# Both inputs loaded by halves of the batch: partition p holds rows 4p to 4p+3 of each half, and the result is stored in two parts

## The chip, the cores and the metric

One core of one Trainium2 chip. The time is the device time of a run in microseconds (us), without the profiler's own work; 84.16 us before the change (3 runs). A profiled execution has a "span" of its own, about 1.3 us shorter than the time of the run that it belongs to (82.9 us for a run of 84.24), because it starts with the first instruction and ends with the last. All runs quoted are in the fast state, at a granted clock of 1.00.

## The reference

```python
batch, dim = 1024, 4096            # x, y: float32
def reference(x, y, axis):         # axis = -1
    return np.sum((x - y) ** 2, axis=axis).astype(np.float32)
```

33.55 MB are read from HBM, the chip's main memory, and 4 KB are written to it.

## The kernel before

128 partitions (P), R = 8 rows each, N = 8 x 4096 columns per partition. X and Y are tiles in the on-chip memory. SP (SyncE) issues all loads into one queue; DVE (VectorE) subtracts, ACT (ScalarE) squares with a running sum, DVE adds up the sums of the pieces of a row ("parts"). The pieces get shorter towards the end, and the last one is squared on DVE itself, with an earlier part as the start value. The engines and the DMA (the transfers) tell each other of finished work by semaphores: counters that one raises and another waits for. The code is cut at the lines of dots.

```python
xv = x.rearrange("(p r) d -> p (r d)", p=P)      # partition p: rows 8p to 8p+7
yv = y.rearrange("(p r) d -> p (r d)", p=P)
ov = out.rearrange("(p r) -> p r", p=P)          # 8 results, 32 B, per partition
...
xw = [16384, 8192, 5472, 1280, 960, 320, 160]    # widths of the loads, in columns
yw = [16256, 8192, 2624, 2784, 1344, 480, 480, 288]
late, last = 128, 192                            # the last two loads of Y
LATE = 3                                         # the row whose end comes last
...
for j, (c0, c1) in enumerate(ys):
    final = j == len(ys) - 1
    wait_loaded(c1, landed_y[j][1])
    for piece in pieces_of(j, c0, c1):
        sub(*piece)                              # DVE
        ...
        if final:                                # DVE: square, add the start value, sum
            nc.vector.tensor_tensor_reduce(..., scalar=parts_of(r, 1),
                accum_out=results[:, r : r + 1]).then_inc(sums, 1)
            continue
        square(*piece, where[piece])             # ACT
        ...
    if j == 4:
        for r in (4, 5, 6):
            complete(r)                          # DVE: sum of the row's parts
complete(7)

nc.sync.wait_ge(sums, n["sums"])
nc.sync.dma_start(out=ov, in_=results).then_inc(stored, 16)
prog.close(nc.sync, stored, 16)                  # SP waits for the store
```

Of the kernel before, what the change touches and what calls it, by code (L numbers as in the profile page):

```python
# [47 lines left out]
def kernel(tc, x, y, axis, out):  # L48
    nc = tc.nc
    P = nc.NUM_PARTITIONS  # L50
    F32 = mybir.dt.float32
    Square = mybir.ActivationFunctionType.Square
    mult, add = mybir.AluOpType.mult, mybir.AluOpType.add

    B, D = x.shape
    R = B // P
    N = R * D


    xv = x.rearrange("(p r) d -> p (r d)", p=P)  # L60
    yv = y.rearrange("(p r) d -> p (r d)", p=P)
    ov = out.rearrange("(p r) -> p r", p=P)


    H = 6 * D
    X = nc.alloc_sbuf_tensor("X", [P, H], F32).ap()
    Y = nc.alloc_sbuf_tensor("Y", [P, H], F32).ap()
    results = nc.alloc_sbuf_tensor("results", [P, R], F32).ap()



    xw = [16384, 8192, 5472, 1280, 960, 320, 160]
    yw = [16256, 8192, 2624, 2784, 1344, 480, 480, 288]
    late, last = 128, 192
    LATE = 3
    halved = (1, 2, 3, 4)
    cut = (LATE + 1) * D - late
    assert sum(xw) == N and sum(yw) == N - late - last
    xs, c = [], 0
    for w in xw:  # L80
        xs.append((c, c + w))
        c += w
    ys, c = [], 0
    for w in yw:
        ys.append((c, c + w))
        c += w
        if c == cut:
            c += late
    ys += [(N - last, N), (cut, cut + late)]

    prog = Program(nc, tc)
    stored = nc.alloc_semaphore("stored")
    diffs = prog.semaphore("diffs")
    acts = prog.semaphore("acts")
    sums = prog.semaphore("sums")
    n = dict(diffs=0, acts=0, sums=0)

    def home(c0, c1):
        h0 = c0 % H
        return slice(h0, h0 + c1 - c0)  # L100


    landed_x, landed_y = [], []
    freed = []

    def load(landed, src, dst, name, c0, c1):
        sem = prog.semaphore("%s%d" % (name, len(landed)))
        nc.sync.dma_start(out=dst[:, home(c0, c1)], in_=src[:, c0:c1]).then_inc(sem, 16)  # L108
        landed.append(((c0, c1), sem))

    order = []
    have = 0
    for c0, c1 in ys:
        while have < c1:
            order.append((landed_x, xv, X, "x") + xs[len([o for o in order if o[3] == "x"])])
            have = order[-1][5]
        order.append((landed_y, yv, Y, "y", c0, c1))

    todo = list(order)
    for _ in range(2):  # L120
        load(*todo.pop(0))
    prog.early(mybir.EngineType.SP)
    while todo and todo[0][5] <= H:
        load(*todo.pop(0))


    row_parts = [[] for _ in range(R)]
    def pieces_of(j, c0, c1):

        pieces = []  # L130
        while c0 < c1:
            e = min(c1, (c0 // D + 1) * D)
            if j in halved:
                h = (c0 + e) // 64 * 32
                pieces.append((c0, h))
                c0 = h
            pieces.append((c0, e))
            c0 = e
        return pieces

    for j, (c0, c1) in enumerate(ys):
        for piece in pieces_of(j, c0, c1):
            row_parts[piece[0] // D].append(piece)
    parts, where = None, {}
    total = sum(len(p) for p in row_parts if len(p) > 1)
    parts = nc.alloc_sbuf_tensor("parts", [P, total], F32).ap()
    k = 0
    for r, p in enumerate(row_parts):
        for piece in p:
            where[piece] = parts[:, k : k + 1] if len(p) > 1 else results[:, r : r + 1]  # L150
            k += len(p) > 1
    first = {}
    k = 0
    for r, p in enumerate(row_parts):
        if len(p) > 1:
            first[r] = k
            k += len(p)

    def parts_of(r, m):
        return parts[:, first[r] : first[r] + m]  # L160

    seen_x = [0]

    def wait_loaded(c1, ysem):

        waits = []
        while seen_x[0] < len(xs) and xs[seen_x[0]][0] < c1:
            waits.append(seen_x[0])
            seen_x[0] += 1
        nc.vector.wait_ge(ysem, 16)  # L170
        for k in waits:
            nc.vector.wait_ge(landed_x[k][1], 16)

    def sub(c0, c1):
        a = X[:, home(c0, c1)]
        nc.vector.tensor_sub(out=a, in0=a, in1=Y[:, home(c0, c1)]).then_inc(diffs, 1)  # L176
        n["diffs"] += 1

    def square(c0, c1, acc):
        a = X[:, home(c0, c1)]  # L180
        nc.scalar.wait_ge(diffs, n["diffs"])
        nc.scalar.activation(out=a, in_=a, func=Square, accum_out=acc).then_inc(acts, 1)  # L182
        n["acts"] += 1

    squared = {}

    def complete(r):
        nc.vector.wait_ge(acts, squared[row_parts[r][-1]])
        nc.vector.tensor_reduce(  # L189
            out=results[:, r : r + 1],  # L190
            in_=parts_of(r, len(row_parts[r])),
            axis=mybir.AxisListType.X,
            op=add,
        ).then_inc(sums, 1)
        n["sums"] += 1
# [5 lines that stand above are left out]
            sub(*piece)  # L201
            r = piece[0] // D
            if final:
                nc.vector.wait_ge(diffs, n["diffs"])
                nc.vector.tensor_tensor_reduce(  # L205
                    out=Y[:, home(*piece)],
                    in0=X[:, home(*piece)],
                    in1=X[:, home(*piece)],
                    scale=1.0,
                    scalar=parts_of(r, 1),  # L210
                    op0=mult,
                    op1=add,
                    accum_out=results[:, r : r + 1],
                ).then_inc(sums, 1)
                n["sums"] += 1
                continue
            square(*piece, where[piece])
            squared[piece] = n["acts"]
            if r in (0, 1):

                nc.sync.wait_ge(acts, n["acts"])  # L221
                while todo and todo[0][5] <= H + (r + 1) * D:
                    load(*todo.pop(0))
                if r == 1:
                    while todo:
                        load(*todo.pop(0))
        if j == 4:
            for r in (4, 5, 6):
                complete(r)
    complete(7)  # L230

    nc.sync.wait_ge(sums, n["sums"])
    nc.sync.dma_start(out=ov, in_=results).then_inc(stored, 16)
    prog.close(nc.sync, stored, 16)


# [33 lines left out]
```

## Time and profile before

| | before |
|---|---|
| time, median of 3 | 84.16 us (84.10 to 84.48) |
| span of the profiled run | 82.9 us |
| DMA share of the span, 16 engines | 95.8% |
| last load landed (trace) | 80.53 us |
| final store issued, landed | 81.47, 82.87 us |

The prediction shows the lines of the profile and reads them. Its times from single DMA records (80.55, 82.89, and with it 1.42 for the store) lie up to 0.02 us above the zero of the profile's views; here they are given from that zero, and the store takes 1.41 us.

One more line matters later. After it has issued the store, SP clears its semaphores and waits for the store's completion. In the view of SP's own waits of the kernel before (columns: us in total, times, longest):

```profile
SPq L45 <- SPq L45: 1.0, 1, 1.0
```

So of the store's 1.4 us, 1.0 is spent in plain waiting at the very end of the program.

### The profile page before, as it was taken

The numbers are of one execution on the slowest core, as the hardware profiler recorded it, in microseconds if no ns is written. First come the engines' busy times: TensorE is split into PE (matmuls) and PEld (weight loads), VectorE is DVE, ScalarE is ACT, GpSimd is POOL, SyncE is SP. The second block draws the span as 40 slices with busy tenths as digits, with TensorE's granted clock in tenths as the row PEclk, the third lists the DMA queues.
The fourth block names the chain that finished last, engine by engine and source line by source line (L and its number), as shares of the span: only waits on it lengthen the run. The fifth ranks groups of instructions, "written<-read, shape, count | busy, mean of one in ns | idle before, by whom it ended". The sixth has DMA issues, their size and how long they took to land.

```text
span 82.9 us, 135 instructions
## 1 busy us (share of the span) xinstructions
DVE 36.9 (44%) x27; ACT 33.5 (40%) x41; POOL 0.2 (0%) x4
## 2 busy tenths in 40 slices
DVE  0000000000000000000299999999189996989992
ACT  0500000000000000000000979889886999899991
POOL 0000000000000000000000000000000000000000
DMA  9299999957999996599799979969989899999960
GB/s 506 95 411 506 506 506 506 474 221 316 502 502 502 502 502 282 220 502 502 316 443 506 427 332 506 490 269 506 411 348 496 369 405 438 430 403 421 396 214 2
DMA packets 2592, 33.56 MB, mean 405 GB/s; under 512 B 416, under 2 KB 1312, under 8 KB 1696
## 3 DMA queue, kind: packets, MB, share of 16 engines
q1 hardware_dynamic: 2592, 33.56, 95.8%
HBM read 33.55 MB, written 0.00 MB: 405 GB/s over the span
## 4 chain that ended last, share of the span: by engine, by line
DMA 64%; SPq 17%; DVE 12%; ACT 4%; issue 1%
DMA Y<-in_y_dram 64%; SPq L108 17%; DVE X L176 11%; ACT X L182 4%; DVE Y L205 0%; DVE results L189 0%; SPq L221 0%; DVE results L205 0%
## 5 line engine op out<-in xcount | busy, mean ns | idle before, releaser
L176 DVE TENSOR_TENSOR X<-X,Y 128x2048 f32<-128x2048 f32 (+10 forms) x21 | 36.3, 1779 | 44.5 <-DMA Y<-in_y_dram 44.4
L182 ACT ACTIVATE X<-X 128x2048 f32<-128x2048 f32 (+9 forms) x20 | 31.2, 1559 | 45.9 <-DVE X L176 45.8
L182 ACT ACTIVATION_READ_ACCUMULATOR X<-X 128x1 f32 x20 | 3.7, 186 | 0.0
L182 ACT ACT_TABLE_LOAD x1 | 1.3, 1283 | 1.9 <-PEq L19 1.9
L189 DVE TENSOR_REDUCE results<-parts 128x1 f32<-128x2 f32 (+2 forms) x4 | 0.4, 151 | 0.0
L205 DVE CUSTOM_DVE_ANT_0 Y<-X,parts 128x128 f32<-128x128 f32 x1 | 0.4, 353 | 0.0
L251 POOL MEMSET const-bfloat16-1.0<- 128x1 bf16 x1 | 0.1, 101 | 0.0
L251 POOL MEMSET const-uint8-127<- 128x1 uint8 x1 | 0.1, 101 | 0.0
L251 POOL MEMSET const-float32-0.0<- 128x1 f32 x1 | 0.1, 98 | 0.2 <-issue 0.2
L251 POOL MEMSET const-float32-1.0<- 128x1 f32 x1 | 0.1, 98 | 0.0
L205 DVE DVE_READ_ACCUMULATOR2_ANT results<- 128x1 f32 x1 | 0.1, 84 | 0.0
## 6 DMA issues: line engine op xcount, KB each, us to landing
Y<-in_y_dram SPq DMA_DIRECT2D x1, 8128.0 KB, 40.6
X<-in_x_dram SPq DMA_DIRECT2D x1, 4096.0 KB, 48.8
Y<-in_y_dram SPq DMA_DIRECT2D x1, 4096.0 KB, 58.2
X<-in_x_dram SPq DMA_DIRECT2D x1, 2736.0 KB, 13.4
Y<-in_y_dram SPq DMA_DIRECT2D x1, 1392.0 KB, 19.0
Y<-in_y_dram SPq DMA_DIRECT2D x1, 1312.0 KB, 16.2
Y<-in_y_dram SPq DMA_DIRECT2D x1, 672.0 KB, 21.2
X<-in_x_dram SPq DMA_DIRECT2D x1, 640.0 KB, 20.1
```

The costliest lines, as they stand in the source:

```text
L108: nc.sync.dma_start(out=dst[:, home(c0, c1)], in_=src[:, c0:c1]).then_inc(sem, 16)
L176: nc.vector.tensor_sub(out=a, in0=a, in1=Y[:, home(c0, c1)]).then_inc(diffs, 1)
L182: nc.scalar.activation(out=a, in_=a, func=Square, accum_out=acc).then_inc(acts, 1)
L189: nc.vector.tensor_reduce(out=results[:, r : r + 1], in_=parts_of(r, len(row_parts[r])), axis=mybir.AxisListType.X, op=add,).then_inc(sums, 1)
L205: nc.vector.tensor_tensor_reduce(out=Y[:, home(*piece)], in0=X[:, home(*piece)], in1=X[:, home(*piece)], scale=1.0, scalar=parts_of(r, 1), ...
L251: nc = _bacc.Bacc("TRN2", target_bir_lowering=False, num_devices=1)
```

## The change

The loads' pieces of a partition are to lie closer together in memory: the 16,384 columns that a partition gets from the first load of X and of Y are four whole rows, and those of partition p+1 now follow at once, so such a load reads 8 MB in one piece. The price is that the results of a partition are two runs (stretches of consecutive bytes) of 4 values, 16 B, rather than one of 8, 32 B. The first half is therefore stored ahead, behind the loads in the queue. With it row 5's end comes last in place of row 3's, for row 3 belongs to the half that is stored early.

```diff
-    xv = x.rearrange("(p r) d -> p (r d)", p=P)
-    yv = y.rearrange("(p r) d -> p (r d)", p=P)
-    ov = out.rearrange("(p r) -> p r", p=P)
+    M = N // 2
+    xv = x.rearrange("(h p r) d -> p h (r d)", h=2, p=P)
+    yv = y.rearrange("(h p r) d -> p h (r d)", h=2, p=P)
+    ov = out.rearrange("(h p r) -> h p r", h=2, p=P)
...
-    yw = [16256, 8192, 2624, 2784, 1344, 480, 480, 288]
-    LATE = 3
+    yw = [16384, 8064, 2624, 2784, 1344, 480, 480, 288]
+    LATE = 5
...
-        nc.sync.dma_start(out=dst[:, home(c0, c1)], in_=src[:, c0:c1]).then_inc(sem, 16)
+        nc.sync.dma_start(out=dst[:, home(c0, c1)], in_=src[:, c0 // M, c0 % M : c0 % M + c1 - c0]).then_inc(sem, 16)
...   # complete(r) and the final square: row 5's start value is the sum of its two earlier parts
+            if r == R // 2 - 1:
+                nc.sync.wait_ge(acts, n["acts"])
+                nc.sync.dma_start(out=ov[0], in_=results[:, 0 : R // 2]).then_inc(stored, 16)
         if j == 4:
             for r in (4, 5, 6):
                 complete(r)
+            nc.vector.wait_ge(sums, n["sums"])
...
-    nc.sync.dma_start(out=ov, in_=results).then_inc(stored, 16)
-    prog.close(nc.sync, stored, 16)
+    nc.sync.dma_start(out=ov[1], in_=results[:, R // 2 : R]).then_inc(stored, 16)
+    prog.close(nc.sync, stored, 32)
```

More of the change, by code (lines that the diff above doesn't have):

```diff
@@ L187, in complete @@
     def complete(r):
-        nc.vector.wait_ge(acts, squared[row_parts[r][-1]])
+        done = row_parts[r][:-1] if r == LATE else row_parts[r]
+        nc.vector.wait_ge(acts, squared[done[-1]])
         nc.vector.tensor_reduce(
-            out=results[:, r : r + 1],
-            in_=parts_of(r, len(row_parts[r])),
+            out=where[row_parts[r][-1]] if r == LATE else results[:, r : r + 1],
+            in_=parts_of(r, len(done)),
             axis=mybir.AxisListType.X,
@@ L209 @@
                     scale=1.0,
-                    scalar=parts_of(r, 1),
+                    scalar=where[piece],
                     op0=mult,
```

## The prediction

> **What bounds the kernel now.** I read four views of the profile, in this order: the page's shares and slices, the chain that ended last, the busy time by stretches of 2 us, and the order of time for the last 4 us.
>
> The page first. It shows whether an engine or the transfers fill the span.
>
> ```profile
> DVE 36.9 (44%) x27; ACT 33.5 (40%) x41; POOL 0.2 (0%) x4
> ...
> q1 hardware_dynamic: 2592, 33.56, 95.8%
> HBM read 33.55 MB, written 0.00 MB: 405 GB/s over the span
> ```
>
> No engine is busy for half of the span; the 16 DMA engines are for 95.8% of it. While busy they moved 405 / 0.958 = 423 GB/s. There is one queue and the inputs are read once, so there are no bytes to save.
>
> The chain says the same, and where the transfers stop setting the end:
>
> ```profile
> 0.43 40.58 DMA Y<-in_y_dram
> ...
> 67.69 12.66 DMA Y<-in_y_dram
> 80.34 0.02 issue
> 80.37 0.57 DVE X L176 x2
> 80.94 0.03 issue
> 80.96 0.35 DVE Y L205
> 81.32 0.01 DVE results L205
> 81.33 0.11 DVE results L189
> ```
>
> Between the two DMA lines the chain runs through compute and through the queue's issue. That part is not what bounds: the third X load was issued at 53.63, when the fourth Y load was still running (DVE waited for it until 60.52). So the queue had about 7 us of work left, and the DMA engines never ran dry. The end is transfers until 80.34, then about 1.1 us of DVE, then the store.
>
> The stretches (columns: length, busy us of DVE, ACT, POOL, clock, DMA share, GB/s):
>
> ```profile
> 8.00:10.00 2.00, 0.00 (x0) 0.00 (x0) 0.00 (x0) 1.00 1.21 524
> 28.00:30.00 2.00, 0.00 (x0) 0.00 (x0) 0.00 (x0) 1.00 1.20 520
> 48.00:50.00 2.00, 2.00 (x2) 1.37 (x3) 0.00 (x0) 1.00 0.91 393
> ```
>
> A transfer is booked by its records' own times, 2.4 us for 64 KB, so a 2 us stretch can show over 1; the quotient is what counts: 524/1.21 = 433, 520/1.20 = 433, 393/0.91 = 432 GB/s. The rate while busy is the same with the compute engines idle and with them busy. Single packet records agree: one of 65,536 bytes takes 2.42 us, 27.1 GB/s per engine, 433 for 16. Smaller packets fit bytes / 27.08 GB/s plus about 7.5 ns (5,120 B in 196 ns, 1,280 B in 55, 512 B in 27).
>
> What falls short of that line, summed over records and divided by 16 engines, is small: the first packet of each engine takes about 3.1 us in place of 2.42 (0.63 us), and some packets from 51 to 63 us take 5 to 19% longer (0.19 us per engine).
>
> The last 4 us:
>
> ```profile
> 78.25 0.27 DVE L189 TENSOR_REDUCE results<-parts 128x1 f32<-128x2 f32 x3
> ...
> 78.44 2.49 DVE L176 TENSOR_TENSOR X<-X,Y 128x480 f32<-128x480 f32 x5
> ...
> 80.96 0.35 DVE L205 CUSTOM_DVE_ANT_0 Y<-X,parts 128x128 f32<-128x128 f32 x1
> 81.06 0.18 ACT L182 ACTIVATION_READ_ACCUMULATOR X<-X 128x1 f32 x1
> 81.24 0.08 DVE L205 DVE_READ_ACCUMULATOR2_ANT results<- 128x1 f32 x1
> 81.28 0.16 DVE L189 TENSOR_REDUCE results<-parts 128x1 f32<-128x8 f32 x1
> 81.47 0.35 SPq L233 DMA_DIRECT2D out_dram<-results  x1
> ```
>
> DVE's last subtractions follow the landings (5 between 78.44 and 80.94, each starting within about 0.1 us of its load). The store is issued at 81.47 and lands at 82.89, 1.42 us later.
>
> **What the Trainium skill says.** (1) "DMA: Bandwidth & Descriptors", section "Bandwidth" (Where 436 GB/s comes from): 16 SBUF ports of 32 B at 850 MHz give 435 GB/s, and 16 MB loaded at 425. The trace agrees: 433 in steady state. If that ceiling is on the SBUF side, no order of the HBM addresses can raise it. (2) The same page, "Latency and other measured facts", row on HBM row pitch: with 16 KiB per partition, copies keep 207 GB/s per direction at a pitch of 512 KiB (214 being full) and lose at 2 MiB and above. It says nothing of 128 or 64 KiB; the trace shows no loss at 128 KB, so I expect none at 64 KB. (3) The same page, "Anatomy of one DMA": the end of a transfer is mostly the receipt of the write, not the bytes. The store of 4 KB with 1.42 us from issue to landing, its packets 7 to 9 ns each, agrees. (4) The same page, "Queues, rings and completion order": an engine consumes descriptors in ring order, and the semaphore's write waits for that engine's earlier writes only. A store queued behind the last load thus cannot hold up that load's semaphore; no run here shows it yet.
>
> **The change part by part.**
>
> *Addresses of the loads.* Bytes do not change: the Y loads are 16,384 and 8,064 columns in place of 16,256 and 8,192; their sum, 24,448, and all later widths stay. Packets: still 17 loads of 128, one per partition, none above 65,536 B. By the fit a load packet costs the same: change 0.00 us for the steady part. What can move is the 0.63 us of the first packets and the 0.19 us of slow ones. The first I take as start-up latency, which addresses don't alter. The second could be bank conflicts between the 16 engines. Then denser addresses may help: a saving of perhaps half, 0.1 us, or up to about 0.4 us if the engine that ends last had most of it (the last load's 16 completions are spread over 80.16 to 80.55).
>
> *First Y load 128 columns wider.* 65,536 against 65,024 B at 27.08 GB/s: lands 0.02 us later per packet, times 8 packets per engine, 0.15 us. DVE's start moves from 41.03 to 41.18. Its fourth subtraction is 4,096 wide (4.42 us) in place of 3,968 (4.28): +0.14. DVE had 2.19 us idle before 60.52, so both vanish; the second X and Y loads end at the same byte count, 49,024 columns, as before. The release of the third X load is 0.15 us later out of 7 us of slack. Two halves of row 5 become 1,984 in place of 2,048 wide: about 0.13 us less before DVE waits for the next load at 70.20. On the path: 0.
>
> *Row 5's end last, in place of row 3's.* The last load has 128 columns as before. One reduction of two parts for row 5 stays, but it writes a part rather than a result. The final fused square-and-sum reads that as its start value. Same count of instructions on the path: 0.57 + 0.35 + 0.11 us as before.
>
> *The new wait of DVE for its own reductions.* Before, the reductions of 78.25 to 78.52 overlap the next subtraction (starting 78.44). Now that must wait for the last reduction's semaphore: about 78.52 plus 0.05, so 0.13 us late. Carried on: subtraction of 480 columns (0.66) ends at 79.23, the next at 79.89 (79.78 before), that of 288 (0.46) at 80.35; the 192-column load lands at 80.36. The delay is used up 0.01 us before the path starts. Cost 0, at worst 0.1.
>
> *The store in two.* The first half is issued after all loads are (they are out at 67.69 + 3.36 = 71.05) and after row 3's squares, which ended at about 62. So its issue at about 71.1, some 0.35 us, or a few us if the queue is still full, is over long before 81.47. It adds 128 packets of 16 B, 8 per engine at about 9 ns, 0.07 us, behind the last load's. They run at about 80.3 to 80.7, while DVE works. The final store has 128 packets still, of 16 B rather than 32: 0.00, with perhaps ±0.1 for short writes sharing a line of memory. Waiting for 32 rather than 16 costs nothing, since the first half has landed by then (estimate: 80.6 + about 1 us = 81.6, before 82.9).
>
> Sum on the path: 0 (steady transfers) − 0.1 (conflicts) + 0 (DVE) + 0 (stores) = −0.1 us, from 84.16: **84.05 us**.
>
> **The rivals.** *A: the layout wins noticeably.* Reading 8 MB in one contiguous piece could remove all the slow packets and part of the start: at most 0.4 + 0.6 = 1.0 us, 83.1 us, 1.2%. For it: the slow packets exist, and the change seems made for it. Against it: over 90% of packets already sit at one duration to 0.1%, the mark of a fixed limit, not of memory conflicts. Even all of it stays inside 2%. *B: the denser pitch hurts.* 16 engines then read at steps of 4 partitions, 256 KB in place of 512 KB. If these met in fewer banks, a loss of 3% in the rate would be 2.4 us, 86.5 us. Against it: the skill's row has losses grow with the pitch, not shrink. *C: a contiguous source is cut into other packets.* If the first loads were merged and cut otherwise, packets and engines would change. Against it: the store before is contiguous on the HBM side as well, and ran as 128 packets of 32 B. *D: the tail gets longer.* If DVE's new wait reaches the last load, or the two stores meet, 0.1 to 0.4 us more: 84.2 to 84.5 us.
>
> **Range and chances.** Before ran from 84.10 to 84.48, so one median carries about 0.15 us. With −0.4 for a good part of A and +0.4 for D, the range is 83.6 to 84.5 us. Over 2% faster means below 82.5 us: 1.6 us less, more than all losses that I could find: 0.03. Over 2% slower means above 85.8, only B or C: 0.03. Within 2%: 0.94.
>
> **What would show it.** Right: DMA share near 96%; quotient of GB/s and share near 433; 2,720 packets (128 more); DVE waiting for the fourth Y load until about 60.5; the last load's wait ending at about 80.3; about 1.1 us of DVE behind it; a final store of about 1.4 us. Wrong: first packets clearly under 3.1 us, or a landing of the second Y load well before 60.5 (A); 64 KB packets over 2.45 us (B); another count of packets (C); the 192-column subtraction starting after its landing, or a final store of over 1.5 us (D).

## The result, and the profile after

The changed kernel is correct and takes 85.12 us in the median (84.97 to 85.55, 4 runs); before took 84.31 us in the same rounds. The ratio is 1.0106, 95% interval 1.0059 to 1.0154. A ratio here is the mean time of one kernel's fast runs over that of the other's of the same rounds, so not quite the ratio of the medians. It is a loss of 1%: "within 2%" holds, but the time lies above the predicted range (83.6 to 84.5).

The page of the changed kernel, lines as in the prediction:

```profile
DVE 36.9 (44%) x27; ACT 33.5 (40%) x41; POOL 0.2 (0%) x4
...
q1 hardware_dynamic: 2736, 33.56, 94.9%
HBM read 33.55 MB, written 0.00 MB: 401 GB/s over the span
```

The same work, and a lower share of DMA because the span (83.6 us) is longer. The packets are 144 more than before: 128 short writes and 16 completions (the prediction's 2,720 left out the 16). In the stretches (same columns as in the prediction)

```profile
8.00:10.00 2.00, 0.00 (x0) 0.00 (x0) 0.00 (x0) 1.00 1.21 524
28.00:30.00 2.00, 0.00 (x0) 0.00 (x0) 0.00 (x0) 1.00 1.21 524
48.00:50.00 2.00, 2.00 (x2) 1.38 (x3) 0.00 (x0) 1.00 0.68 295
```

the quotient is 433, 433 and 434 GB/s: the loads run at the same rate. (The low share in the last line comes of how packets fall into a 2 us stretch; the quotient is not touched by that.) The chain that ended last:

```profile
0.43 40.67 DMA Y<-in_y_dram
...
67.64 12.66 DMA Y<-in_y_dram
80.30 0.02 issue
80.32 0.57 DVE X L178 x2
80.89 0.02 issue
80.92 0.35 DVE Y L209
81.27 0.01 DVE results L209
81.28 0.15 DVE results L193
```

It ends at 81.43, before at 81.44. In order of time, the last of it:

```profile
78.25 0.14 DVE L193 TENSOR_REDUCE parts<-parts 128x1 f32<-128x2 f32 x1
...
78.31 0.14 DVE L193 TENSOR_REDUCE results<-parts 128x1 f32<-128x4 f32 x1
78.49 2.39 DVE L178 TENSOR_TENSOR X<-X,Y 128x480 f32<-128x480 f32 x5
...
81.27 0.16 DVE L193 TENSOR_REDUCE results<-parts 128x1 f32<-128x8 f32 x1
81.46 0.34 SPq L242 DMA_DIRECT2D out_dram<-results  x1
```

The final store is issued at 81.46, before at 81.47. Up to here the two kernels are level to 0.01 us, and all that is lost must lie behind this line. It does. The DMA issues after 81 us (columns: count, KB, median us from issue to landing), first of the kernel before, then of the changed one:

```profile
out_dram<-results SPq DMA_DIRECT2D x1, 4.0 KB, 1.4
```

```profile
out_dram<-results SPq DMA_DIRECT2D x1, 2.0 KB, 2.2
```

and SP's last wait in the changed kernel, 1.0 us before:

```profile
SPq L45 <- SPq L45: 1.7, 1, 1.7
```

A store of half the bytes takes longer. The trace's single records tell which part of it: the 128 packets and 16 completion packets of the final store run from 82.31 to 82.51 us before and from 82.29 to 82.50 us after, each 7 to 9 ns long in both. But the 16 completions, at which the semaphore counts up, arrive from 82.72 to 82.87 before, and from 82.70 to 83.61 after. So the store's time splits into issue to first packet, packets, and last packet to last completion: 0.85, 0.20 and 0.37 us before, 0.84, 0.20 and 1.11 us after. The packets are sent as fast as ever; it is the confirmation of some of the writes that comes late. The 0.74 us by which the last completion moved are the 0.7 us of the span.

### The profile page after: what moved, and what is told of

Its sections match the earlier page's. It is cut to its first block, busy times and chain, and to the rows that moved or that the text cites. A ratio compares the mean times of both kernels' runs of the same rounds, so it can differ in the third digit from the quotient of the medians.

```text
span 83.6 us, 136 instructions
## 1 busy us (share of the span) xinstructions
DVE 36.9 (44%) x27; ACT 33.5 (40%) x41; POOL 0.2 (0%) x4
## 4 chain that ended last, share of the span: by engine, by line
DMA 64%; SPq 17%; DVE 12%; ACT 4%; issue 1%
DMA Y<-in_y_dram 64%; SPq L110 17%; DVE X L178 11%; ACT X L184 4%; DVE Y L209 0%; DVE results L193 0%; SPq L225 0%; DVE results L209 0%
## 5 line engine op out<-in xcount | busy, mean ns | idle before, releaser
L178 DVE TENSOR_TENSOR X<-X,Y 128x4096 f32<-128x4096 f32 (+10 forms) x21 | 36.2, 1779 | 44.5 <-DMA Y<-in_y_dram 44.3
L184 ACT ACTIVATE X<-X 128x4096 f32<-128x4096 f32 (+9 forms) x20 | 31.2, 1559 | 45.8 <-DVE X L178 45.6
```

The costliest lines, as they stand in the source:

```text
L178: nc.vector.tensor_sub(out=a, in0=a, in1=Y[:, home(c0, c1)]).then_inc(diffs, 1)
L184: nc.scalar.activation(out=a, in_=a, func=Square, accum_out=acc).then_inc(acts, 1)
```

## The experiments

Theory S: the short runs of the final store are the cause, by their length or by how many lie close together. Theory T: the second store suffers from the first, which ran 2 us ahead of it. Theory L: the loads' addresses, or the new order of the rows, cost time after all. In the table below, "tail" is the time from the end of the final store's last packet to its last completion, from the records of the trace of one profiled run. The ratios are to the kernel before, run on the same chip in the same call. The numbered parts below take the runs in turn; the text in quotes is what was expected before each ran.

| run | final store: runs of, placed | short writes per 256 B | tail, us | ratio (95%) |
|---|---|---|---|---|
| before | 32 B, dense | 8 | 0.37 | 1 |
| before_again | 32 B, dense | 8 | 0.37 | 1.0012 (0.9997 to 1.0026) |
| order_and_wait_only | 32 B, dense | 8 | 0.37 | 1.0019 (1.0006 to 1.0032) |
| loads_only | 32 B, dense | 8 | 0.37 | 1.0027 (1.0005 to 1.0048) |
| old_loads_split_store | 16 B, step 32 B | 8 | 0.37 | 1.0029 (1.0007 to 1.0050) |
| pairs_step_64 | 16 B, 2 per 64 B | 8 | 0.37 | 1.0071 (1.0045 to 1.0096) |
| fours_step_128 | 16 B, 4 per 128 B | 8 | 0.49 | 1.0077 (1.0064 to 1.0090) |
| eights_step_256 | 16 B, 8 per 256 B | 8 | 0.51 | 1.0103 (1.0085 to 1.0121) |
| the changed kernel | 16 B, dense | 16 | 1.11 | 1.0106 (1.0059 to 1.0154) |
| final_half_alone | 16 B, dense | 16 | 1.20 | 1.0138 (1.0114 to 1.0162) |
| dense_far_engines | 16 B, dense, permuted | 16 | 1.31 | 1.0164 (1.0140 to 1.0188) |
| sixteens_step_512 | 16 B, 16 per 512 B, permuted | 16 | 1.12 | 1.0162 (1.0145 to 1.0179) |
| one_store_256_runs | 256 of 16 B, dense | 16 | 1.44 | 1.0157 (1.0131 to 1.0184) |
| dense_8_bytes | 8 B, dense | 32 | 1.94 | 1.0181 (1.0148 to 1.0215) |

The count per 256 B supposes that the output starts at a multiple of 256 B, which the trace does not show. In sixteens_step_512, eights_step_256 and the like the count is that of the filled stretches.

### 1. loads_only

```diff
-    ov = out.rearrange("(h p r) -> h p r", h=2, p=P)
+    ov = out.rearrange("(p r) -> p r", p=P)            # results in a wrong order, on purpose
-                nc.sync.dma_start(out=ov[0], in_=results[:, 0 : R // 2])...   # and its wait
-    nc.sync.dma_start(out=ov[1], in_=results[:, R // 2 : R])...
+    nc.sync.dma_start(out=ov, in_=results)...          # one store, as before
```

> New load addresses, row 5's end last and the wait of DVE, but one store of 32 B runs as before (so the results land in a wrong order, on purpose). If the lost 0.8 us is all in the final store (my theory after the two traces), this runs like the kernel before: ratio 0.995 to 1.003, the store lands 1.4 to 1.5 us after its issue. If the loads' addresses or the new order cost time, it stays at about 1.01.

84.37 us against 84.16: 1.0027, inside what was expected. With the new loads and the old form of the store, SP's last wait is what it was before:

```profile
SPq L45 <- SPq L45: 1.0, 1, 1.0
```

So the loads don't hold the 1%: theory L falls as the main cause. Experiment 6 looks at the 0.27% that are left.

### 2. final_half_alone

```diff
-                nc.sync.dma_start(out=ov[0], in_=results[:, 0 : R // 2])...   # and its wait
-    prog.close(nc.sync, stored, 32)
+    prog.close(nc.sync, stored, 16)                    # half of the result not written, on purpose
```

> The changed kernel without its first store (half of the result is not written, wrong on purpose); the final store still has 128 runs of 16 B in 2 KB. Theory S (short runs: 16 B writes are slow in themselves or by sharing a line): slow as the changed kernel, ratio about 1.01, completions of the final store spread over 0.5 us or more. Theory T (the second store suffers from the first one 2 us ahead of it): like before, ratio about 1.00, spread under 0.2 us.

85.36 us, 1.0138. The wait at the end, without any first store:

```profile
SPq L45 <- SPq L45: 1.8, 1, 1.8
```

The completions spread over 0.99 us. Theory T falls: the slow store needs no store ahead of it. (In this profiled run the last load also landed 0.3 us later than in most; the tail, 1.20 us, doesn't contain that.)

### 3. old_loads_split_store

```diff
-    xv = x.rearrange("(h p r) d -> p h (r d)", h=2, p=P)                  # and yv
+    xv = x.rearrange("(p r) d -> p (r d)", p=P)
-    ov = out.rearrange("(h p r) -> h p r", h=2, p=P)
+    ov = out.rearrange("(p h r) -> h p r", h=2, p=P)   # 16 B at a step of 32 B
```

> The load addresses of before with the store still in two: 16 B runs at a step of 32 B, so that each store touches all 4 KB. Right result. Theory S by length (each write under 32 B is slow): about 1.01. Theory S by crowding (four runs in one 64 B, all in 2 KB): half of the crowding, ratio 1.000 to 1.006. Theory T: about 1.01, because a first store is there as well.

Correct, 84.37 us, 1.0029. Two stores of 128 runs of 16 B, as in the changed kernel, and yet

```profile
SPq L45 <- SPq L45: 1.0, 1, 1.0
```

The length of a run is thus not the cause: 16 B at a step of 32 B land like 32 B. What is left of theory S is the crowding. This kernel is the changed one with the crowding taken away, and it is correct; it does not beat the kernel before.

### 4. one_store_256_runs

```diff
-    ov = out.rearrange("(h p r) -> h p r", h=2, p=P)
+    ov = out.rearrange("(h p r) -> p h r", h=2, p=P)   # first store taken out
-    nc.sync.dma_start(out=ov[1], in_=results[:, R // 2 : R])...
+    nc.sync.dma_start(out=ov, in_=results.rearrange("p (h r) -> p h r", h=2))...
```

> The changed loads with one final store of both halves: 256 runs of 16 B over 4 KB, right result. Theory S by length with a fixed time for each write: twice the loss, 1.6 us, ratio about 1.02. Theory S by crowding: as the changed kernel or a little more, 1.01 to 1.015. Theory T: no first store, so only the added 8 packets of 9 ns per engine: ratio about 1.001.

Correct, 85.45 us, 1.0157. The tail grows to 1.44 us: more than the changed kernel's 1.11, not double the loss. Each form of theory S that was written down missed by a little: by length would have been 1.02, by crowding at most 1.015. It lies closer to crowding, and with experiment 3 only that is left. Its last wait:

```profile
SPq L45 <- SPq L45: 2.1, 1, 2.1
```

Splitting the store in two probably helps, given this layout, as it hides one half. It is not shown: the intervals of the two ratios overlap (1.0131 to 1.0184 here, 1.0059 to 1.0154 for the changed kernel), and each tail is from one profiled run.

### 5. How close is too close: six stores

Five runs of this series store the last four results of each partition alone, with the new loads (wrong on purpose), and differ only in where the 16 B runs go; dense_8_bytes stores two results.

```diff
 # pairs_step_64, fours_step_128, eights_step_256: g = 2, 4, 8 runs dense, then as much left empty
-    ov = out.rearrange("(h p r) -> h p r", h=2, p=P)
+    ov = out.rearrange("(a f) -> a f", f=8*g)[:, 0:4*g].rearrange("a (b r) -> a b r", b=g)
 # dense_far_engines: dense, partition 8a+b at place 16b+a
+    ov = out.rearrange("(h b a r) -> h a b r", h=2, a=16, b=8)
 # sixteens_step_512: 16 dense, then 256 B empty, partition 8a'+b' permuted in the same way
+    ov = out.rearrange("(a f) -> a f", f=128)[:, 0:64].rearrange("a (b r) -> b a r", b=16)
 # dense_8_bytes: 8 B runs, dense in 1 KB
+    ov = out[0 : 2 * P].rearrange("(p r) -> p r", p=P)
```

> As final_half_alone (new loads, only a final store of 128 runs of 16 B, wrong on purpose), but the runs lie in pairs: two fill one aligned 32 B, the next 32 B stay empty. Two runs per 64 B, as in old_loads_split_store, which lost nothing. Theory of the 32 B piece (a second write into the same 32 B must wait for the first): loss of 0.4 to 1.0 us against before, completions spread over 0.4 us or more. Theory of the count per 64 B (more than two writes per 64 B are slow) or of the area (2 KB rather than 4 KB): no loss beyond the 0.2 us of loads_only, spread under 0.2 us.

pairs_step_64: the tail is 0.37 us, as before. Two neighbours in one 32 B do not hurt each other; the theory of the 32 B piece falls. The ratio of 1.0071 has another reason: from issue to landing this store takes 1.85 us, not 1.41. The issue of a store with two steps on the memory side takes SP 0.64 us, not 0.35, and another 0.15 us pass before the first packet; the rest of the ratio is like that of loads_only. The last wait is 1.1.

```profile
81.39 0.64 SPq L241 DMA_DIRECT2D out_dram<-results  x1
```

```profile
SPq L45 <- SPq L45: 1.1, 1, 1.1
```

So for these patterns the tail is to be compared, or the ratio only among runs with the same 0.64 us of issue.

> As final_half_alone, dense runs of 16 B in 2 KB, but partition 8a+b writes place 16b+a, so that neighbours in memory come from partitions 8 apart[...]. If the writes collide at the memory, whoever sends them: still slow, ratio about 1.01 (1.008 to 1.018). If the collision is between writes that one engine sends one behind the other to one place: ratio 1.000 to 1.005, spread under 0.25 us.

dense_far_engines: 1.0164, tail 1.31 us. Moving neighbours to partitions 8 apart does not help, and the issue takes 0.64 us here too, so the longer issue of pairs_step_64 is not what made that one fast. Which DMA engine sends which partition the trace does not show; whether neighbours came from one engine or from several is therefore not shown either.

> As final_half_alone, but 128 runs of 8 B, dense in 1 KB: four per 32 B in place of two. Theory of the 32 B piece: three of four writes must wait rather than one of two, so the loss over loads_only grows from about 0.8 us to 1.2 us or more, ratio 1.017 to 1.03. If the loss is a fixed one for any dense store of under 32 B: 1.010 to 1.015.

dense_8_bytes: 1.0181, tail 1.94 us for 1 KB.

```profile
SPq L45 <- SPq L45: 2.6, 1, 2.6
```

The loss in the tail over 0.37 is 1.57 us, twice that of the dense 16 B runs (0.74 to 0.83). A fixed loss falls: the denser, the slower. Its expectation was written for the 32 B piece, which pairs_step_64 had refuted in the same call; the growth came, its reason was another.

> As pairs_step_64 (a final store of 128 runs of 16 B alone, wrong on purpose, over 4 KB), but the runs lie in fours that fill one aligned 64 B, the next 64 B empty. If more than two writes per 64 B is what is slow: last landing 0.8 us or more after the last packet (0.37 where nothing is lost), ratio 1.012 or more, 0.3 us of it for the longer issue. If it is the writes per larger stretch of memory (the same number over 4 KB in place of 2 KB): landing 0.37 to 0.5 us after the last packet, ratio 1.005 to 1.009, as pairs_step_64.

fours_step_128: tail 0.49 us; four writes into one 64 B cost about 0.12 us, not the 0.74 of the changed kernel. Writes per 64 B are not the main thing. The ratio, 1.0077, is in the range given for the larger stretch.

> The same with eights that fill 128 B, the next 128 B empty. By writes per 64 B: as slow as fours_step_128. If fours_step_128 is fast and this slow, the stretch that matters is 128 B. If both are fast, it is larger still.

eights_step_256: tail 0.51 us, so a full 128 B isn't it either.

```profile
SPq L45 <- SPq L45: 1.3, 1, 1.3
```

The profiled run was the fastest of four here (84.77 us; the others 85.01 to 85.25), so its tail may be below the usual one.

> A final store of 128 runs of 16 B alone (wrong on purpose) over 4 KB: sixteen runs fill 256 B, the next 256 B stay empty; neighbours come from partitions 8 apart, as in dense_far_engines, which landed 1.31 us after its last packet. If the stretch that takes only so many writes at a time is 256 B: as slow, 1.0 us or more from the last packet to the last landing. If it is larger still, or the whole 4 KB counts: 0.4 to 0.6 us, as fours and eights (0.49, 0.51).

sixteens_step_512: tail 1.12 us, SP's last wait

```profile
SPq L45 <- SPq L45: 1.9, 1, 1.9
```

With 256 B filled by 16 writes the whole loss is there, although half of the 4 KB stays empty, as with the eights. Sorted by the number of short writes per 256 B, all fourteen stores fall in line: 8 gives a tail of 0.37 to 0.51 us, 16 gives 1.11 to 1.44, 32 gives 1.94. Two limits of this: the sixteens were also permuted, which the eights were not (in dense stores that made 1.31 out of 1.20), and each tail is from one profiled run. The times of all runs agree, though: with the same issue, the eights have a ratio of 1.0085 to 1.0121, the sixteens of 1.0145 to 1.0179. And why 256 B counts these runs do not show.

### 6. order_and_wait_only and before_again

```diff
 # order_and_wait_only: the changed kernel with the loads and the single store of before
-    xv = x.rearrange("(h p r) d -> p h (r d)", h=2, p=P)                  # and yv
+    xv = x.rearrange("(p r) d -> p (r d)", p=P)
-    ov = out.rearrange("(h p r) -> h p r", h=2, p=P)                      # and the two stores
+    ov = out.rearrange("(p r) -> p r", p=P)
```

> Load addresses of before and one store of 32 B runs; only row 5's end in place of row 3's, with it the two widths and DVE's wait. Right result. Both loads_only and old_loads_split_store, which share this part, were 0.27 to 0.29% over before. If this part costs it: ratio 1.002 to 1.004. If it is nothing (my prediction's zero for this part): 0.999 to 1.001.

> The kernel before against itself, as a control for differences of a quarter of a per cent: ratio 0.999 to 1.001. If it comes out at 1.002 or more, the 0.27% of the other runs is not to be told from how the runs are taken.

The control, the kernel before against itself, came out at 1.0012 (84.21 us against 84.15), the order alone at 1.0019 (84.30). Both miss the ranges that were written down by a little: the control stays under the 1.002 that would have put the whole 0.27% down to how the runs are taken, and the order's interval leaves out 1. But the two intervals overlap, so whether the order costs about 0.1% stays open. The profile shows a small thing. The chain that ended last of before_again, then of order_and_wait_only:

```profile
67.65 12.66 DMA Y<-in_y_dram
80.31 0.02 issue
80.33 0.57 DVE X L176 x2
...
81.28 0.12 DVE results L189
```

```profile
78.43 0.07 DVE results L193
...
78.53 0.67 DVE X L178
...
79.22 2.06 ACT X L184 x8
...
81.31 0.16 DVE results L193
```

In this run with DVE's new wait the chain no longer comes through the last load, but from DVE's reductions at 78.4 through ACT, which works without a gap (2.06 us for 8 instructions) to the end. The last reduction starts at 81.31 in place of 81.24 in these two executions, in the changed kernel's own, whose chain still comes through the last load, at 81.27. It is at most 0.07 us, and no run's time resolves it.

## Why the prediction was wrong

**The bound and the loads: right.** 433 GB/s while busy, before and after; no load cut into packets other than its width gives; DVE waited for the fourth Y load until 60.43 (predicted about 60.5); the last load landed at 80.48. The Trainium skill's ceiling ("DMA: Bandwidth & Descriptors", section "Bandwidth") held: nothing was to be had from these addresses.

**The saving of 0.1 us from bank conflicts: not there.** The slow packets that I had read as a property of the addresses (0.19 us per engine by the fit) change from one execution to the next. The same kernel profiled again, before_again, had 0.05 us of them by the same count that gives 0.29 for the first profile (single records against the usual time of their size, first packets left out). The changed kernel's profile had 0.16, and of two runs with its loads loads_only had 0.06 and final_half_alone 0.29. The first packets cost 0.61 us per engine after and 0.70 to 0.80 us in the two profiles of before (the prediction's 0.63 is 0.70 by this count), a difference no larger than that of the two. Rival A falls with it.

**The wider first Y load, row 5's end, DVE's wait: right in their sum.** DVE's next subtraction began at 78.49 rather than the 78.57 expected, and the store was issued at 81.46, as before. What the working overlooked is that ACT's chain runs level with DVE's there (in order_and_wait_only it ends last, at 81.29), so that ACT has no slack to take a delay up.

**The first store behind the loads: right.** Its issue took 3.52 us at 71.04, which I read as a full queue, as the prediction allowed; its completions came from 80.31 to 80.64 us, long before the final store. The last load's landed from 80.13 to 80.48, within the range of the runs without a first store (the last at 80.46 in loads_only, 80.49 in before_again, 80.82 in final_half_alone), which agrees with what the skill says on ring order.

**The final store: the step that failed.** The prediction put it as "128 packets still, of 16 B rather than 32: 0.00, with perhaps ±0.1 for short writes sharing a line of memory". It measured 0.74 us in the trace: 1.41 us from issue to the last completion became 2.15. I had counted packets, and these did stay the same (0.20 us of packets in both). What changed was the time from the last packet to the last completion, 0.37 to 1.11 us, and experiment 5 shows that it follows from where in memory the short writes lie: with the same loads and the same 128 runs of 16 B it is 0.37 us for pairs and 1.20 us dense. "Sharing a line of memory" thus named the right place, if a stretch of 256 B is meant, and gave it too little. The sign was among rival D's ("a final store of over 1.5 us"), but D's causes were not the ones: DVE's wait did not move the store's issue, and the two stores do not meet, for final_half_alone has the same late completions without a first store. D's size was guessed at "0.1 to 0.4" with no duration behind it, because the trace held only one store, in one form. Point (3) of the prediction set the receipt of the write beside the whole 1.42 us; of the time only 0.37 us came after the last packet, and that is the part that grew. The skill had warned of short writes, on the same page, section "Specifications": it puts the least size for full rate at 512 B and says that below it a read-modify-write is done. I passed over that row, since 32 B was as far below it as 16 B; and by that row alone the two would indeed be equal.

From 84.05 to 85.12: 0.1 us of saving that was not there, 0.15 us because before itself ran at 84.31 in these rounds rather than 84.16, and about 0.8 us of the final store. The last figure is what remains (1.07 − 0.1 − 0.15); the profiled run, the fastest of the four, shows 0.74 of it.

## What to carry to other kernels

When a layout is changed for the sake of the loads, look at what it does to the last store: its confirmation lies on the path with nothing beside it, and many short writes packed into a few hundred bytes were confirmed later here than the same number spread out, at equal packet time. Read a store from its issue to its last completion, not by its packets. Before a few slow packets are called a property of the addresses, profile the same kernel twice.

## What the Trainium skill lacked or had wrong

- "DMA: Bandwidth & Descriptors", section "Specifications": the row on the least transfer for full rate speaks of size only. Here runs of 16 B at a step of 32 B were confirmed as fast as runs of 32 B (0.37 us after the last packet); dense ones took 1.11 to 1.44 us and dense ones of 8 B 1.94 us. The number of short writes per 256 B ordered all stores tried: 8, 16, 32.
- The same page, section "Anatomy of one DMA": the fixed part, given as about 2.0 us and as scaling with nothing, is fitted to DMAs issued from GpSimd. From SP, a store of 4 KB took 1.41 us from issue to landing, one of 2 KB with denser runs 2.15 us, one of 1 KB 3.0 us, so it is not constant here. The page also puts most of the fixed part down to the receipt of the write. In the kernel before, the time after the last packet was 0.37 of the 1.41 us, and 0.85 us lay before the first packet; in the dense stores it is half (1.11 of 2.15) to two thirds (1.94 of 3.0).
- I found no page that tells how the issue time on SP depends on the form of the pattern: 0.35 us for a store with one step per partition, 0.64 us for the same 128 runs placed with two steps, 0.40 us for 256 runs with partitions outermost.
- On the row about the pitch of partitions in HBM ("Latency and other measured facts", same page): no loss at 128 and 64 KB, which it does not list; 433 GB/s at both.
